# Feed-forward gate and up products as seven half-size products instead of eight, with the sums of weights on VectorE, and the down product in two groups

## The chip, the cores and the metric

The kernel runs on one core of a Trainium2 chip, as one program. The metric is device time in microseconds, lower is better. The engines are named as in the profile: PE is TensorE (its weight loads are listed as PEld), DVE is VectorE, ACT is ScalarE, POOL is GpSimd, SP issues the DMAs.

## The reference, cut to what matters

Two stacks of layers follow each other on 512 tokens of width 1024. They hold six feed-forward stages, two in the first stack (called ff0 and ff1 here) and four in the second (b0f1, b0f2, b1f1, b1f2), and between these mixers and a cross-attention. Only the feed-forward stages change.

```python
x = x + swiglu(rmsnorm(x, norm_ffn_g[layer]), ffn_w_gate_up[layer], ffn_w_down[layer])        # ff0, ff1
...
def _swiglu(h, w_gate, w_up, w_down):
    return (jax.nn.silu(h @ w_gate) * (h @ w_up)) @ w_down
...
x = x + 0.5 * _swiglu(_rmsnorm(x, ffn1_norm[i]), ffn1_w_gate[i], ffn1_w_up[i], ffn1_w_down[i])   # b0f1, b1f1
...
x = x + 0.5 * _swiglu(_rmsnorm(x, ffn2_norm[i]), ffn2_w_gate[i], ffn2_w_up[i], ffn2_w_down[i])   # b0f2, b1f2
```

The inner width is 2816 in all six, that is 22 column blocks of 128 for gate, 22 for up, and 22 blocks of rows for down.

## The kernel before

Rows are kept transposed: 8 chunks of 128 features by 512 tokens. A product in full precision is made of three matmuls: each operand is split into a rounded part and the rest (`split`, line 752: ScalarE makes the rounded copy `hi`, VectorE subtracts it to give `lo`), and hi by hi, hi by lo and lo by hi are summed in PSUM. The weights are split on the chip too: `weights` (line 765) loads a block of 128 x 8 x 128 floats (1024 columns per partition) into one of 3 tiles `raw`, then one ScalarE copy and one VectorE subtraction of 1024 columns fill two of the 6 tiles `part`.

`dense` (line 799) makes one column block: 8 chunks by 3 matmuls, each with 512 moving columns, so 24 matmuls. `ffn` (line 989) goes over the 22 inner blocks j: gate block j, then up block j, and in between `gate` for the block before, which scales both by the norm's factors, takes the silu, multiplies, and splits the result (4 VectorE instructions of 512 columns, the three products and the subtraction). The 22 pairs that come out are the operands of down: 8 column blocks of 22 x 3 = 66 matmuls, by `residual` (line 963), each added to a chunk of the rows by `add_product`. `prepare` (line 934) makes of every finished chunk what the next stage's norm takes from it. The last stage's down is `last_residual` (line 1025): its last column block goes by two halves of 256 tokens, so that the final norm of the first half runs under the products of the second.

The order of issue is not the order of the code. `Plan` collects the whole program and `schedule` (line 487) lists it anew, so that each engine takes the first instruction that could start by a model of the engines' times, with the tiles of each kind (line 655: 64 `blk` of 512 words, 3 `raw`, 6 `part`, 8 PSUM banks) as a limit. Each engine then runs its own list strictly in that order, waiting on semaphores. All instructions are issued from line 640 (in the changed kernel line 648), so rows are told apart by tile shape.

Of the kernel before, what the change touches and what calls it, by code (L numbers as in the profile page):

```python
# [28 lines left out]


# ---------------------------------------------------------------- host side: layout only
def _lay(w):
    """[K, N] -> [N/128, 128, K/128, 128]: one stationary column block per row of DRAM."""
    k, n = w.shape
    return np.ascontiguousarray(w.reshape(k // P, P, n // P, P).transpose(2, 1, 0, 3))


def _mov(w, kc):
    """[K, 512] -> [K/128/kc, 128, kc, 512]: moving blocks."""
    k, n = w.shape  # L40
    return np.ascontiguousarray(w.reshape(k // P // kc, kc, P, n).transpose(0, 2, 1, 3))

# [70 lines left out]
def _hyena_constants():  # L113
# [11 lines left out]
    # token order: even tokens, then odd ones  # L125
# [3 lines left out]
    # half-bin shifted frequencies: theta = 2 pi (f + 1/2) / 1024  # L129
# [4 lines left out]
    # forward: stationary [t, f]; [fc][128 t, (mat, kc), 128 f]  # L134
# [13 lines left out]
def pack(inputs):  # L148
# [9 lines left out]
    for l in range(2):  # L158
# [6 lines left out]
        a[f"ff_d{l}"] = _lay(g["ffn_w_down"][l])  # L165
# [66 lines left out]
class View:  # L232
    """A view of a Store, made when its memory is known; lo and hi bound the elements it can touch."""
# [64 lines left out]
class Plan:  # L298
    """Takes the program's instructions in an order that is right, and issues them in one in which each engine
    takes the first instruction, by that order, of those that could start, by a model of the engines' times.  # L300
    An instruction is taken ahead of others only where the tiles that it needs leave what is in front of it
    enough of them in any case."""
# [7 lines left out]
    def __init__(self, tc, kinds):  # L310
        """kinds: kind -> (pool, number of tiles, words per partition)"""
# [15 lines left out]
    def ahead(self, n=400):  # L327
        """what is added meanwhile comes before what it otherwise would by n instructions"""
# [30 lines left out]
    # ---- the program  # L359
# [47 lines left out]
    def _time(self, op, outs, ins):  # L407
        """microseconds on the engine"""
# [5 lines left out]
        if op.engine == "tensor":  # L414
# [3 lines left out]
            if rhs.dtype != F32:  # L418
                return 0.003 + max(size(rhs), 2 * P if rhs.dtype == F32R else 64) / 2400.0
# [18 lines left out]
    # ---- the order  # L438
# [2112 lines left out]
```

## Time and profile before

| | us |
|---|---|
| median of 3 runs | 3643.41 |
| lowest and highest run | 3643.01, 3643.46 |
| span of the profiled execution, first to last instruction | 3643.5 |
| PE busy in it | 3596.1 |
| DVE busy | 2042.3 |
| ACT busy | 1350.5 |
| POOL busy | 290.4 |

The profiled execution's own time is its span, 3643.5 us; nothing lies around it that the runs would count, since they agree with it within 0.5 us. Busy times count an instruction from its start to its end, and the starts of neighbours on one engine overlap the ends a little.

### The profile page before, as it was taken

To read this page: it belongs to the slowest core of one execution; us is meant where nothing else is said; L and a number is where in the kernel's file an instruction comes from. 1 tells how busy PE (TensorE), PEld (TensorE's weight loads), DVE (VectorE), ACT (ScalarE), POOL (GpSimd) and SP (SyncE) were. 2 spreads that over 40 slices of the span, in tenths; PEclk is the share of its full clock that TensorE was granted. 3 is DMA by queue.
4 is the path that set the end of the run, shared out by engine and by line. 5 is a ranking of instruction groups with operands and counts; after the bars stand their busy time and mean duration, and the time that the engine had idled before them with its cause. 6 is when DMAs were issued, how large, how long until landed. Compare 5 with 4: busy or idle time off the path is not lost. (4 is left out here: it accounts for less than half of the span.)

```text
span 3643.5 us, 46845 instructions
## 1 busy us (share of the span) xinstructions
PE 3596.1 (99%) x18186; PEld 2949.0 (81%) x18186; DVE 2042.3 (56%) x3262; ACT 1350.5 (37%) x2166; POOL 290.4 (8%) x358
## 2 busy tenths in 40 slices
PE   9999999999999999999999999999999999999998
PEld 6888888778788888887878888888888778888887
DVE  7664434466744345435887854434442787774433
ACT  4353223354532332222554442222322455443221
POOL 2010001000100010003210010000000330010000
PEclk9999999999999999999999999999999999999999
DMA  5323233233232322333425433333333432822232
GB/s 165 116 79 100 93 97 94 75 124 105 77 115 93 97 93 94 99 111 117 144 94 198 157 120 94 96 96 97 98 107 97 138 123 93 291 86 93 94 97 81
DMA packets 157654, 404.20 MB, mean 111 GB/s; under 512 B 17326, under 2 KB 40911, under 8 KB 157432
## 3 DMA queue, kind: packets, MB, share of 16 engines
q1 hardware_dynamic: 157432, 401.21, 34.6%
q8 instruction: 143, 2.34, 0.3%
q14 instruction: 79, 0.65, 0.1%
HBM read 375.46 MB, written 25.69 MB: 110 GB/s over the span
## 5 line engine op out<-in xcount | busy, mean ns | idle before, releaser
L640 PE MATMUL t<-t,t 128*128 128x512 f32 (+4 forms) x16892 | 3498.8, 367 | 28.4 <-ACT t L640 14.4
L640 PEld LDWEIGHTS t<-t,t 128*128 128x128 f32 (+1 forms) x15484 | 2766.9, 189 | 613.7 <-issue 28.5
L640 DVE TENSOR_TENSOR t<-t,t 128x512 f32<-128x512 f32 (+11 forms) x1831 | 1465.4, 813 | 1318.1 <-PE t L640 1102.9
L640 ACT CAST t<-t 128x1024 fp32r<-128x1024 f32 (+4 forms) x998 | 828.8, 841 | 1981.6 <-PE t L640 1481.6
L640 POOL TENSOR_TENSOR t<-t,t 128x512 f32<-128x512 f32 (+1 forms) x139 | 191.9, 1387 | 2169.6 <-ACT t L640 1806.6
L640 ACT ACTIVATE t<-t 128x512 f32<-128x512 f32 (+7 forms) x331 | 173.8, 534 | 79.4 <-DVE t L640 54.6
L640 DVE SCALAR_TENSOR_TENSOR t<-t,f,t 128x512 f32<-128x512 f32 (+2 forms) x209 | 155.8, 753 | 10.3 <-ACT t L640 7.1
L640 PE MATMUL t<-f,t 128*128 128x128 f32 (+2 forms) x1008 | 137.6, 258 | 11.0 <-DVE t L640 7.5
L640 PEld LDWEIGHTS t<-f,t 128*128 128x128 f32 (+1 forms) x880 | 113.1, 173 | 24.1 <-DVE t L640 6.9
L640 ACT COPY t<-t 128x512 f32<-128x512 f32 (+3 forms) x155 | 83.0, 558 | 109.4 <-PE t L640 107.4
L640 DVE SCALAR_TENSOR_TENSOR t<-f,f,t 128x512 fp32r<-128x512 f32 (+2 forms) x104 | 90.3, 885 | 52.4 <-ACT t L640 49.8
L640 POOL MEMSET t<- 128x2 f32 (+4 forms) x159 | 29.0, 214 | 1072.5 <-DVE t L640 540.7
L640 ACT ACTIVATE t<-t,t 128x128 f32<-128x128 f32 (+3 forms) x248 | 89.4, 435 | 42.9 <-PE t L640 26.6
L640 PEld LDWEIGHTS <-t 128*128 128x128 f16 (+1 forms) x1550 | 70.3, 98 | 40.6 <-issue 20.0
L640 DVE TENSOR_TENSOR f<-t,f 128x512 f32<-128x512 f32 x64 | 44.0, 688 | 56.6 <-PE t L640 56.6
L640 DVE SCALAR_TENSOR_TENSOR f<-t,f 128x512 f32<-128x512 f32 (+1 forms) x33 | 22.3, 676 | 94.2 <-PE t L640 94.2
L640 DVE SCALAR_TENSOR_TENSOR t<-t,t 128x4 f32<-128x4 f32 (+10 forms) x175 | 64.8, 377 | 13.3 <-ACT t L640 9.8
L640 ACT ACTIVATE t<-f 128x512 f32<-128x512 f32 (+1 forms) x105 | 64.4, 618 | 17.9 <-DVE f L640 17.2
L640 ACT ACTIVATE t<-t,f 128x512 f32<-128x512 f32 (+2 forms) x101 | 63.8, 657 | 13.2 <-PE t L640 10.8
L640 ACT ACTIVATE t<-f,f 128x512 fp32r<-128x512 f32 (+1 forms) x80 | 57.0, 718 | 29.0 <-DVE f L640 27.1
L640 DVE SCALAR_TENSOR_TENSOR t<-t,t,t 128x128 f32<-128x128 f32 x192 | 55.2, 345 | 11.8 <-PE t L640 8.5
L640 DVE TENSOR_TENSOR t<-t,f 128x512 f16<-128x512 f32 (+5 forms) x77 | 47.3, 623 | 5.7 <-PE t L640 5.2
(37 smaller groups left out, 421.2 us busy)
## 6 DMA issues: line engine op xcount, KB each, us to landing
t<-d SPq DMA_DIRECT2D x232, 256.0 KB, 4.7
t<-in_ffn_g SPq DMA_DIRECT2D x88, 512.0 KB, 3.5
t<-in_ffn_u SPq DMA_DIRECT2D x88, 512.0 KB, 3.4
t<-in_ffn_d SPq DMA_DIRECT2D x64, 512.0 KB, 3.6
t<-in_ff_g SPq DMA_DIRECT2D x44, 512.0 KB, 3.5
t<-in_ff_u SPq DMA_DIRECT2D x44, 512.0 KB, 3.5
d<-t SPq DMA_DIRECT2D x88, 256.0 KB, 3.3
t<-in_ff_d SPq DMA_DIRECT2D x32, 512.0 KB, 3.5
```

The lines of the kernel that those rows point to most:

```text
L640: ins = getattr(getattr(nc, o.engine), o.fn)(*[got(v) for v in o.args], **{k: got(v) for k, v in o.kw.items()})
```

## The change

The gate weights are taken two column blocks at a time, j and j + 11, together with the two halves of the 1024 features (chunks 0 to 3, and 4 to 7), and the tokens in two halves of 256 (`L` and `R`). A product of two such 2 x 2 arrangements of blocks takes eight block products when it is written out; here it is written with seven, of sums and differences of the blocks (the scheme is Strassen's, in Winograd's form). So `seven` issues 7 products of 4 chunks by 3 matmuls, 84 matmuls with 256 moving columns each, for what were two column blocks of 24 matmuls with 512 columns each. The same is done for up.

The sums on the side of the rows are made once per stage: `combine` makes 7 operands of chunk i and chunk i + 4. The sums of the weights are made for each pair of blocks by `combined_weights`: 4 additions of 512 columns on VectorE, and the split of 3584 columns where two blocks had 2048. Sums of the products: ScalarE copies four partial results out of PSUM, and VectorE adds them in `gate`. Down goes in two groups of inner rows, 12 blocks after j = 5 and 10 after j = 10 (`GROUPS`), each with its own 8 additions to the rows; its matmuls are the same ones as before. The host lays the rows of the down weights in the order in which the pairs come out (`_down`). There are 4 tiles `raw` in place of 3, and 63 `blk` in place of 64. The planner's time of a matmul has a new formula, so its lists change somewhat elsewhere too. Lines that are only comments are gone.

```diff
+GROUPS = [(0, 6), (6, 5)]
...
+def _down(w):
+    order = [k for i in range(FC // 2) for k in (i, FC // 2 + i)]
+    return np.ascontiguousarray(_lay(w)[:, :, order, :])
...
-            a[f"{f}_d{l}"] = _lay(g[f"{f}_w_down_2"][l])
+            a[f"{f}_d{l}"] = _down(g[f"{f}_w_down_2"][l])
...
-            "blk": (sb, 64, T), "raw": (sb, 3, 2 * T), "part": (sb, 6, 2 * T), "pad": (sb, 4, T + 16),
+            "blk": (sb, 63, T), "raw": (sb, 4, 2 * T), "part": (sb, 6, 2 * T), "pad": (sb, 4, T + 16),
...
-        if c == 0:
-            self.pre = {"xs": []}
+        if self.pre is None:
+            self.pre = {"xs": [None] * DC, "rows": {}}
...
-        if kind != "squares":
+        if kind == "xs":
             hi, lo = self.pair()
-            self.split_scaled(self.x[c], pre["g12"][:, c:c + 1] if kind == "twice" else self.col(g[0], g[1] + c), hi, lo)
-            pre["xs"].append((hi, lo))
+            self.split_scaled(self.x[c], self.col(g[0], g[1] + c), hi, lo)
+            pre["xs"][c] = hi, lo
+        elif kind != "squares":
+            row = pre["rows"][c] = self.blk()
+            nc.scalar.activation(out=row, in_=self.x[c], func=AF.Copy,
+                                 scale=pre["g12"][:, c:c + 1] if kind == "twice" else self.col(g[0], g[1] + c))
+            i = c % 4
+            if {i, i + 4} <= set(pre["rows"]):
+                pre["xs"][i] = self.combine(pre["rows"].pop(i), pre["rows"].pop(i + 4))
...
+    def combine(self, b1, b2):
+        nc = self.nc
+        L, R = slice(0, 256), slice(256, 512)
+        sub = lambda out, a, b: nc.vector.tensor_tensor(out=out, in0=a, in1=b, op=ALU.subtract)
+        minus = lambda out, a, b: nc.vector.scalar_tensor_tensor(out=out, in0=a, scalar=-1.0, in1=b, op0=ALU.mult,
+                                                                 op1=ALU.subtract)
+        one = self.blk(F32R)
+        self.split(b1[:, L], one[:, L], one[:, R])
+        low = self.pair()
+        self.split(b2, *low)
+        ta, tb = self.blk(), self.blk()
+        sub(ta[:, L], b1[:, L], b1[:, R])
+        minus(ta[:, R], b2[:, R], ta[:, L])
+        sub(tb[:, L], b2[:, R], b1[:, R])
+        minus(tb[:, R], ta[:, R], b2[:, L])
+        pa, pb = self.pair(), self.pair()
+        self.split(ta, *pa)
+        self.split(tb, *pb)
+        half = lambda pr, s: (pr[0][:, s], pr[1][:, s])
+        return [(one[:, L], one[:, R]), half(low, L), half(low, R), half(pb, R), half(pa, L), half(pa, R), half(pb, L)]
+    def combined_weights(self, a, b):
+        nc = self.nc
+        L, R = slice(0, T), slice(T, 2 * T)
+        ra, rb, s = (nc.tile("raw", (P, 2 * T)) for _ in range(3))
+        for r, src in ((ra, a), (rb, b)):
+            nc.sync.dma_start(out=r.rearrange("p (k n) -> p k n", n=P), in_=src)
+        add = lambda out, x, y: nc.vector.tensor_tensor(out=out, in0=x, in1=y, op=ALU.add)
+        def parts(src, n, kind="part"):
+            hi, lo = (nc.tile(kind, (P, n), F32R) for _ in range(2))
+            self.split(src, hi, lo)
+            return hi, lo
+        first = parts(ra, 2 * T)
+        add(s[:, R], ra[:, L], rb[:, L])
+        add(rb[:, L], rb[:, L], rb[:, R])
+        add(s[:, L], rb[:, L], ra[:, L])
+        third = parts(s, 2 * T)
+        second = parts(rb, 2 * T)
+        add(ra[:, R], ra[:, R], s[:, L])
+        last = parts(ra[:, R], T, "blk")
+        half = lambda pr, h: tuple(z[:, h].rearrange("p (k n) -> p k n", n=P) for z in pr)
+        return [half(first, L), half(first, R), half(last, L), half(second, R), half(second, L), half(third, L), half(third, R)]
+    def seven(self, w, xs, V, fresh):
+        nc = self.nc
+        bank = self.acc()
+        X, Z = bank[:, 0:256], bank[:, 256:512]
+        def product(out, n, start=False):
+            hi, lo = w[n]
+            mm = [(hi, k, z) for k in range(4) for z in xs[k][n]] + [(lo, k, xs[k][n][0]) for k in range(4)]
+            for i, (part, k, z) in enumerate(mm):
+                go = start and i == 0
+                nc.tensor.matmul(out, lhsT=part[:, k, :], rhs=z, start=go, stop=True, skip_group_check=not go)
+        ea, eb = self.blk(), self.blk()
+        e1, u2, u3, e5 = ea[:, 0:256], ea[:, 256:512], eb[:, 0:256], eb[:, 256:512]
+        product(X, 0, True)
+        nc.scalar.copy(out=e1, in_=X)
+        product(Z, 1)
+        product(X, 5)
+        nc.scalar.copy(out=u2, in_=X)
+        product(V, 4, fresh)
+        nc.scalar.copy(out=e5, in_=V)
+        product(X, 6)
+        nc.scalar.copy(out=u3, in_=X)
+        product(V, 2)
+        product(X, 3)
+        return Z, V, X, e1, u2, u3, e5
...
     def ffn(self, norm, wg, wu, wd, half):
         nc = self.nc
...
+        vt = nc.vector.tensor_tensor
+        minus = lambda out, a, b: nc.vector.scalar_tensor_tensor(out=out, in0=a, scalar=-1.0, in1=b, op0=ALU.mult, op1=ALU.mult)
+        L, R = slice(0, 256), slice(256, 512)
...
+        xs = self.pre["xs"][:4]
+        xs, factors = self.norm(*norm, xs=xs)
+        I = self.I
         rs = None
+        hidden = []
         def gate(G, U):
+            Z, V, X, e1, u2, u3, e5 = G
+            a, b = self.tmp(), self.tmp()
+            vt(out=a[:, L], in0=Z, in1=e1, op=ALU.add)
+            vt(out=a[:, R], in0=V, in1=u2, op=ALU.add)
+            minus(b[:, L], X, rs[:, L])
+            vt(out=b[:, R], in0=u3, in1=e5, op=ALU.add)
+            vt(out=a, in0=a, in1=rs, op=ALU.mult)
+            minus(b[:, R], b[:, R], rs[:, R])
+            for z in (a, b):
+                nc.scalar.activation(out=z, in_=z, func=AF.Silu)
+                vt(out=z, in0=z, in1=rs, op=ALU.mult)
+            Z, V, X, e1, u2, u3, e5 = U
+            h1, h2 = self.blk(), self.blk()
+            vt(out=h1[:, L], in0=Z, in1=e1, op=ALU.add)
+            vt(out=h1[:, R], in0=V, in1=u2, op=ALU.add)
+            minus(h2[:, L], X, b[:, L])
+            vt(out=h2[:, R], in0=u3, in1=e5, op=ALU.add)
+            vt(out=h1, in0=h1, in1=a, op=ALU.mult)
+            minus(h2[:, R], h2[:, R], b[:, R])
+            for z in (h1, h2):
+                pr = self.pair()
+                self.split(z, *pr)
+                hidden.append(pr)
+        def down(g):
+            i0, n = GROUPS[g]
+            ks = slice(2 * i0, 2 * i0 + 2 * n)
+            ys = list(hidden)
+            hidden.clear()
+            coming, self.coming = self.coming, self.coming if g else None
+            if g and self.out is not None:
+                self.last_residual(lambda c: I[wd][c][:, ks, :], ys, half)
+            else:
+                self.residual_with(lambda c: self.dense(None, c, ys, kmax=6, src=I[wd][c][:, ks, :]), half,
+                                   (0, 4, 1, 5, 2, 6, 3, 7))
+            self.coming = coming
+        last, bank = None, None
+        for j in range(FC // 2 + 1):
+            G = U = None
+            if j < FC // 2:
+                bank = self.acc()
+                G = self.seven(self.combined_weights(I[wg][j], I[wg][j + FC // 2]), xs, bank[:, L], True)
+                if j == 0:
+                    next(factors)
             if last is not None:
                 gate(*last)
+            if sum(GROUPS[0]) == j:
+                for _ in range(8):
+                    next(factors, None)
+                down(0)
+            if j < FC // 2:
+                U = self.seven(self.combined_weights(I[wu][j], I[wu][j + FC // 2]), xs, bank[:, R], False)
+                if j == 0:
+                    rs = next(factors)
+                else:
+                    for _ in range(2):
+                        next(factors, None)
+                last = G, U
+        down(1)
...
```

How this stands in the engines' lists. First DVE, in the middle of b0f1. Before, one inner block j takes these six rows (the three tiles with 1024 columns at their end belong to weights; t2177 holds the norm's factors):

```order
L640 TENSOR_TENSOR t2276_11240<-t2258_11139,t2268_11183 128x1024
L640 TENSOR_TENSOR t2279_11253<-t2271_11213,t2177_10655 128x512
L640 TENSOR_TENSOR t2281_11274<-t2265_11177,t2273_11217 128x1024
L640 TENSOR_TENSOR t2284_11287<-t2278_11251,t2177_10655 128x512
L640 TENSOR_TENSOR t2284_11287<-t2284_11287,t2279_11253 128x512
L640 TENSOR_TENSOR t2287_11304<-t2284_11287,t2286_11299 128x512
```

Of the change, in the same stage, from the third weight sum's subtraction (t2706, reading the tile `s`, t2699) to the use of the next set's second weight block (t2709, which SP loads into the tile that t2699 leaves, once t2706 is made):

```order
L648 TENSOR_TENSOR t2706_14240<-t2699_14185,t2703_14220 128x1024
L648 TENSOR_TENSOR t2708_14253<-t2692_14133,t2702_14208 128x1024
L648 TENSOR_TENSOR t2711_14268<-t2676_14007,t2704_14232 128x512
L648 TENSOR_TENSOR t2701_14194<-t2701_14194,t2633_13713 128x512
L648 TENSOR_TENSOR t2696_14149<-t2696_14149,t2633_13713 128x512
L648 TENSOR_TENSOR t2714_14292<-t2694_14142,t2713_14276 128x1024
L648 TENSOR_TENSOR t2716_14306<-t2694_14142,t2709_14257 128x512
L648 TENSOR_TENSOR t2701_14194<-t2701_14194,t2633_13713 128x512
L648 TENSOR_TENSOR t2709_14257<-t2709_14257 128x512
L648 TENSOR_TENSOR t2705_14235<-t2688_14111,t2691_14130 128x256
L648 TENSOR_TENSOR t2716_14306<-t2709_14257,t2694_14142 128x512
L648 SCALAR_TENSOR_TENSOR t2719_14339<-t2688_14111,t2696_14149 128x256
```

Where two subtractions of weights and four instructions of the gate made a block, 32 instructions now make a pair of blocks, 16 of them for weights, and weight sums and gate sums alternate.

Second, PE in the same place. Before, the first chunks of one column block (t2259 is the PSUM tile, t2244 the weights):

```order
L640 MATMUL t2259_11141<-t2043_9825,t2244_11039 128x512
L640 MATMUL t2259_11141<-t2045_9832,t2244_11039 128x512
L640 MATMUL t2259_11141<-t2057_9919,t2244_11039 128x512
L640 MATMUL t2259_11141<-t2059_9926,t2244_11039 128x512
L640 MATMUL t2259_11141<-t2071_10015,t2244_11039 128x512
```

Of the change, the first of seven products (t2677 is `hi` of the weights, from ScalarE, t2678 `lo`, from VectorE; a row with x2 is the two parts of one operand) and the start of the second:

```order
L648 MATMUL t2688_14111<-t2476_12977,t2677_14017 128x256 x2
L648 MATMUL t2688_14111<-t2504_13094,t2677_14017 128x256 x2
L648 MATMUL t2688_14111<-t2533_13219,t2677_14017 128x256 x2
L648 MATMUL t2688_14111<-t2561_13345,t2677_14017 128x256 x2
L648 MATMUL t2688_14111<-t2476_12977,t2678_14033 128x256
L648 MATMUL t2688_14111<-t2504_13094,t2678_14033 128x256
L648 MATMUL t2688_14111<-t2533_13219,t2678_14033 128x256
L648 MATMUL t2688_14111<-t2561_13345,t2678_14033 128x256
L648 MATMUL t2688_14111<-t2487_13027,t2677_14017 128x256
```

Each of the seven is twelve matmuls of half the width, eight with `hi` and then four with `lo`.

Third, DVE at the start of ff0, from the last chunks of the cross-attention's output on (f8 and f9 are chunks 6 and 7 of the rows). Before:

```order
L640 TENSOR_TENSOR f8_81<-t467_2176,f8_81 128x512
L640 TENSOR_TENSOR t477_2218<-t457_2141,t472_2196 128x1024
L640 TENSOR_TENSOR f9_82<-t474_2203,f9_82 128x512
L640 SCALAR_TENSOR_TENSOR t482_2237<-f8_81,f1_74,t476_2214 128x512
L640 SCALAR_TENSOR_TENSOR t485_2250<-f9_82,f1_74,t483_2242 128x512
L640 TENSOR_TENSOR t487_2260<-t464_2166,t475_2207 128x1024
```

Of the change, from behind the eighth matmul of the first product, up to the `lo` weights that its ninth reads (t498):

```order
L648 TENSOR_TENSOR t489_2259<-t482_2234,t486_2247 128x512
L648 SCALAR_TENSOR_TENSOR t457_2136<-t480_2226,t457_2136 128x256
L648 TENSOR_TENSOR t492_2267<-t480_2226,t488_2255 128x512
L648 TENSOR_TENSOR t494_2271<-t480_2226,t448_2107 128x256
L648 SCALAR_TENSOR_TENSOR t494_2271<-t457_2136,t480_2226 128x256
L648 TENSOR_TENSOR t495_2275<-t457_2136,t493_2269 128x512
L648 TENSOR_TENSOR f9_82<-t477_2214,f9_82 128x512
L648 TENSOR_TENSOR t454_2126<-t454_2126 128x512
L648 TENSOR_TENSOR t498_2283<-t445_2096,t465_2162 128x1024
```

Where one instruction prepared each chunk, `combine` now has nine for each pair of chunks, and two of the four pairs come due within the last chunks of the stage before.

## Rows read from the trace of the kernel before

**Rows 1.** The page: busy time of the engines, and their share in 40 slices of the span.
```profile
PE 3596.1 (99%) x18186; PEld 2949.0 (81%) x18186; DVE 2042.3 (56%) x3262; ACT 1350.5 (37%) x2166; POOL 290.4 (8%) x358
...
PE   9999999999999999999999999999999999999998
...
DVE  7664434466744345435887854434442787774433
```
**Rows 2.** What PE waited for, whole span: us in total, times, longest.
```profile
PE t L640 <- DVE t L640: 20.2, 24, 2.4
PE t L640 <- ACT t L640: 15.8, 19, 2.8
```
**Rows 3.** Windows: from:to, length, busy us (x instructions) by engine, clock, DMA.
```profile
400.00:500.00 100.00, 100.00 (x440) 82.24 (x439) 45.29 (x52) 29.98 (x37) 0.21 (x2) 1.00 0.32 98
1000.00:1100.00 100.00, 100.00 (x435) 81.37 (x434) 48.13 (x58) 32.16 (x39) 0.00 (x0) 1.00 0.35 111
1400.00:1500.00 100.00, 100.00 (x435) 81.34 (x434) 47.29 (x55) 29.31 (x36) 0.00 (x0) 1.00 0.29 95
2200.00:2300.00 100.00, 100.00 (x437) 81.85 (x437) 47.57 (x55) 29.76 (x38) 0.00 (x0) 1.00 0.32 98
2600.00:2700.00 100.00, 100.00 (x442) 82.58 (x441) 47.93 (x56) 30.24 (x38) 0.00 (x0) 1.00 0.31 95
3300.00:3400.00 100.00, 100.00 (x442) 82.58 (x441) 48.20 (x55) 29.30 (x36) 0.00 (x0) 1.00 0.29 95
```
**Rows 4.** Timeline of PE: one 256-column matmul, then runs of them (start, length).
```profile
204.17 0.37 PE L640 MATMUL t<-t,t 128*128 128x256 f32 x1
...
3618.09 6.18 PE L640 MATMUL t<-t,t 128*128 128x256 f32 x50
...
3624.70 3.24 PE L640 MATMUL t<-t,t 128*128 128x256 f32 x25
...
3628.14 3.68 PE L640 MATMUL t<-t,t 128*128 128x256 f32 x29
```
**Rows 5.** Timeline of DVE: two neighbours, then unbroken runs of equal instructions.
```profile
1718.98 0.69 DVE L640 TENSOR_TENSOR t<-t,t 128x512 f32<-128x512 f32 x1 [0.18 <-PE t L640]
1719.59 0.74 DVE L640 SCALAR_TENSOR_TENSOR t<-f,f,t 128x512 f32<-128x512 f32 x1
1720.25 2.49 DVE L640 TENSOR_TENSOR t<-t,t 128x512 fp32r<-128x512 f32 x4
...
1951.45 2.36 DVE L640 TENSOR_TENSOR t<-t,t 128x1024 fp32r<-128x1024 f32 x2
...
2011.04 1.09 DVE L640 TENSOR_TENSOR t<-t 128x256 f32<-128x256 f32 x3
```
**Rows 6.** Groups by shape in b0f1's gate and up, 1310 to 1556 us.
```profile
L640 DVE TENSOR_TENSOR t<-t,t 128x1024 fp32r<-128x1024 f32 x43 | 53.6, 1249 | 73.3 <-PE t L640 69.2 <-ACT t L640 4.1
L640 ACT CAST t<-t 128x1024 fp32r<-128x1024 f32 x44 | 46.3, 1053 | 154.0 <-PE t L640 141.2 <-issue 12.7
L640 ACT ACTIVATE t<-t 128x512 f32<-128x512 f32 x20 | 12.5, 624 | 5.1 <-DVE t L640 5.1
L640 ACT CAST t<-t 128x512 fp32r<-128x512 f32 x19 | 11.8, 621 | 9.1 <-DVE t L640 9.1
```
**Rows 7.** DMA issues in the same stretch: count, KB each, median us to landing.
```profile
t<-in_ffn_u SPq DMA_DIRECT2D x22, 512.0 KB, 3.4
t<-in_ffn_g SPq DMA_DIRECT2D x21, 512.0 KB, 3.5
```
**Rows 8.** Windows outside the feed-forward stages in which DVE is busiest.
```profile
1700.00:1800.00 100.00, 94.85 (x442) 73.34 (x442) 87.54 (x150) 50.60 (x83) 34.87 (x43) 1.00 0.35 117
2000.00:2100.00 100.00, 93.76 (x634) 86.43 (x633) 83.31 (x206) 49.68 (x139) 1.30 (x1) 0.95 0.50 167
2900.00:3000.00 100.00, 98.23 (x733) 79.86 (x732) 86.72 (x163) 58.27 (x91) 28.66 (x45) 1.00 0.37 124
```
**Rows 9.** Windows: gate and up of ff0 and of ff1, from their first load on.
```profile
227.00:460.00 233.00, 231.89 (x1022) 190.28 (x1021) 120.06 (x145) 75.86 (x96) 8.28 (x6) 1.00 0.32 100
948.00:1189.00 241.00, 238.67 (x1030) 192.84 (x1029) 131.65 (x171) 84.07 (x106) 9.61 (x8) 0.99 0.33 104
```
**Rows 10.** Timeline of DVE at the end: the norm of the two halves.
```profile
3628.42 3.22 DVE L640 SCALAR_TENSOR_TENSOR t<-f,f,t 128x256 f32<-128x256 f32 x8 [1.22 <-PE t L640]
3631.85 0.42 DVE L640 SCALAR_TENSOR_TENSOR f<-t,f 128x256 f32<-128x256 f32 x1 [0.21 <-PE t L640]
...
3637.29 3.22 DVE L640 SCALAR_TENSOR_TENSOR t<-f,f,t 128x256 f32<-128x256 f32 x8 [1.31 <-PE t L640]
```

More of the change, by code (lines that the diff above doesn't have):

```diff
@@ L964, in residual, with residual_with @@
         self.residual_with(lambda c: self.dense(wname, c, ys, order=order), half)
-    def residual_with(self, product, half):
+    def residual_with(self, product, half, order=range(DC)):
         last = None
-        for c in range(DC):
+        for c in order:
             acc = product(c)
-            if c:
-                self.add_product(c - 1, last, half)
-            last = acc
+            if last is not None:
+                self.add_product(*last, half)
+            last = c, acc
             if self.side is not None:
                 next(self.side, None)
-        self.add_product(DC - 1, last, half)
+        self.add_product(*last, half)
     def add_product(self, c, acc, half, tokens=None):
@@ L1018, in ffn @@
-            last = G, U
-        gate(*last)
-        if self.out is not None:
-            self.last_residual(wd, a, half)
-        else:
-            self.residual(wd, a, half)
-    def last_residual(self, wname, ys, half):
+            if sum(GROUPS[0]) == j:
[10 more added lines that the diff above has]
+                last = G, U
@@ L1028, in last_residual @@
+        down(1)
+    def last_residual(self, weights, ys, half):
         nc = self.nc
@@ L1030, in last_residual, with parts, product @@
         last = None
+        kc = len(ys)
+        def parts(c):
+            return [(k, self.weights(weights(c)[:, k:min(k + 5, kc), :], min(k + 5, kc) - k)) for k in range(0, kc, 5)]
+        def product(out, ws, s):
+            for k0, (hi, lo) in ws:
+                self.mm3s(out, [((hi[:, k, :], lo[:, k, :]), tuple(z[:, s] for z in ys[k0 + k])) for k in range(min(5, kc - k0))],
+                          k0 == 0, k0 + 5 >= kc)
         for c in range(DC - 1):
-            acc = self.dense(wname, c, ys)
+            acc = self.acc()
+            product(acc, parts(c), slice(0, T))
             if c:
@@ L1036, in last_residual @@
         c = DC - 1
-        kc = len(ys)
-        parts = [(k, self.weights(self.I[wname][c][:, k:min(k + 8, kc), :], min(k + 8, kc) - k)) for k in range(0, kc, 8)]
+        w = parts(c)
         self.add_product(c - 1, last, half)
@@ L1042, in last_residual @@
             acc = self.acc()[:, :256]
-            for k0, (hi, lo) in parts:
-                self.mm3s(acc, [((hi[:, k, :], lo[:, k, :]), tuple(z[:, s] for z in ys[k0 + k])) for k in range(min(8, kc - k0))],
-                          k0 == 0, k0 + 8 >= kc)
+            product(acc, w, s)
             with nc.ahead():
@@ L2487, in _coming @@
     if s[2:] in ("f1", "f2"):
-        return "xs", f"ffn{s[3]}_norm_2", int(s[1]) * DC
+        return "xc", f"ffn{s[3]}_norm_2", int(s[1]) * DC
     return ("squares",)
```

46 lines of the change are left out of this document (16 added, 30 removed).

## The prediction

> **What bounds the kernel now.** I read the page first. PE is busy 99% of the span, in every slice but the last, and DVE 56% [rows 1]. Then the waits: PE waited 20.2 us for DVE and 15.8 us for ACT in the whole execution [rows 2]. So the time is the sum of PE's instructions, and an edit helps if it shortens that sum and keeps PE fed. Then six stretches from inside the six gate and up parts: PE is at 100%, DVE at 45 to 48%, ACT at 30%, and the clock at its full level of 2.4 GHz [rows 3]. There PE issues 435 to 442 matmuls of 512 columns in 100 us, on average 438.5, one in 0.228 us.
>
> I count in pairs: two inner blocks, gate and up. There are 11 pairs in a stage and 66 in the kernel. Before, a pair is 2 x 2 x 24 = 96 matmuls of 0.228 us, 21.9 us of PE.
>
> **PE's work.** A pair becomes 2 x 84 = 168 matmuls of 256 columns. Their price stands in the last column block, which already goes by halves. A matmul alone lasts 0.37 us, and a run of 50 lasts 6.18 us, so one starts every (6.18 - 0.37) / 49 = 0.119 us; the runs of 25 and 29 give 0.120 and 0.118 [rows 4]. That is more than half of 0.228: each matmul pays some columns' time whatever its width, and the change pays it 1.75 times as often. A pair is then 168 x 0.119 = 20.0 us. The 512-column rate spreads by 1.6% between stages [rows 3]; the same spread here gives 19.8 to 20.3. The floor of PE falls by 1.9 us a pair, 125 us in all. Down has the same matmuls as before and saves nothing.
>
> The Trainium skill, "TensorE: Matmul & The Clock Gate", section "Back-to-back issue gap", gives N / 2.4 + 2.5 ns, which would be 109 ns for 256 columns and 216 ns for 512, and by it a pair would go from 20.7 to 18.4 us, a saving of 2.4 us. The rows show 119 and 228 ns, so I take 1.9.
>
> **DVE's work.** A neighbour starts 0.61 us after the start of an instruction that lasts 0.69, so an unbroken run ends about 0.08 us later than its last share. Runs of two, four and three then give 1.135 us for 1024 columns, 0.60 for 512 and 0.337 for 256 [rows 5]. Before, a pair cost 4 subtractions of weights and 8 instructions of the gate: 4 x 1.135 + 8 x 0.60 = 9.3 us of 21.9. After, the weights of gate and of up each take three subtractions of 1024, one of 512 and four sums of 512: 6 x 1.135 + 10 x 0.60 = 12.8 us for both. The gate has six instructions of 512 columns and ten of 256: 3.6 + 3.4 = 7.0 us. Together 19.8 us against PE's 20.0. That doubles DVE, and it is the whole risk. The sums in 256 columns with a constant (the `minus` lines) have no row of their own; the nearest, 0.337, is taken, and at the 512-column price they would add at most 1.1 us a pair.
>
> **ACT** rounds 6 x 1.05 us of weights, 2 x 0.62 more, two silus and two roundings of 0.62 each [rows 6], and copies eight pieces of 256 columns out of PSUM, for which no row stands; they cost between nothing and the 0.62 of a 512-column instruction. That is 10 to 15 us of 20: no bound, but each copy stands between two products that share `X` or `V`. Another product of 12 x 0.119 = 1.4 us lies between them and covers a copy of half a microsecond, even behind part of a rounding of 1.05.
>
> **How far PE and DVE can drift apart.** The six `part` tiles hold one set of weights. A tile pair that is last read in the fifth of seven products (7.1 us into a set of 10) is read again in the third product of the next set (at 12.9). In these 5.7 us ACT needs 1.05 and DVE 1.14, so DVE may come some 3 us early or late before PE waits. Within a group of six pairs DVE also starts with its first set done under the stage before, and the gate of the last pair falls under down: it has some 106 us of work (6 x 19.8 less 6.4 and 7.0) for 120 us of PE, but it can use only those 3 us or so of lead. What it loses within a set, waiting for a rounding or a load, it can hardly make up. The second weight block of a set is loaded into the tile that the third sum's subtraction leaves. DVE then has 1.14 + 3 x 0.60 + 1.14 = 4.1 us of other work by its list, and a load lands 3.4 to 3.5 us after its issue [rows 7]: covered, with 0.6 us to spare. If that cover is gone, DVE waits, and then PE. In the same stage before, DVE also waited for ACT, 4.1 us over 43 of the subtractions [rows 6], 0.1 us each.
>
> I take a pair at 20.5 us: the 20.0 of PE, 0.2 for the spread of rates, 0.3 for waits behind DVE. That gives 66 x 1.4 = 92 us. The bounds are 19.8 (DVE's sum alone, PE at its best) and 22.6 (below).
>
> **What the change adds.** At the start of ff0 and ff1 the stage before is short. DVE has there, by its list, from behind the eighth matmul of the first product to the `lo` that the ninth reads, 4 x 0.60 + 3 x 0.337 + 0.60 + 1.14 = 5.1 us, with nothing else for PE. Another 1 us goes for the last chunk's operands. In their gate and up parts PE was idle 1.1 and 2.3 us before [rows 9], mostly at that place, so the net is about 4.4 us each: 9 us. A clock that falls in the gap could add some: in the stretch in which PE was idle for 6.2 us, the mean granted clock was 0.95 [rows 8]. The four other stages start behind products of 5 us and more a column block; there the last chunk's operands (an addition, a ScalarE pass, a rounding, signals) come about 2.8 us after the last product, and two products of half width cover most of that: 1.5 us each, 6 us. Where a group of down begins or ends, PE changes to tiles that the others have just left: 1 us a stage, 6 us. Down's 8 more additions lie on a DVE that is idle there. At the end, the second half's products shrink from 66 matmuls to 30, and the first half's norm, 3.22 us of DVE [rows 10], lies less under them: 2 us. In all 23 us, between 8 and 45.
>
> **Sum.** 3643.5 - 92 + 23 = 3574.5, against an execution that agrees with the median of the runs.
>
> **The rivals.**
> PE at its floor: DVE's lead hides all its waits, and a pair takes 20.0 us or a little less. For it speaks the 5.7 us window; against it that both engines would be at 99%. 3643.5 - 125 + 23 = 3541; 0.14. If the matmuls of 256 columns came faster than 0.119, DVE would bound, at 19.8: 3643.5 - 139 + 23 = 3528. The rows speak against it, 0.02. The formula of the Trainium skill's page on TensorE, named above, would lead there.
>
> DVE paces: it waits 1.2 us a pair for roundings and loads, so the pair takes 21.0 to 21.2. 3643.5 - 53 + 23 = 3614. For it speaks that each engine keeps its list's order and that each of the eight splits of a pair's weights waits for a rounding; 0.17.
>
> Slower than before: DVE can't be kept busier here than where it is busiest now, 83 to 88% in stretches in which PE itself fell to 94 to 98% [rows 8]. 19.8 / 0.875 = 22.6 us a pair, 66 x 0.7 = 46 us lost, and 3643.5 + 46 + 23 = 3713. The point from which it decides is 21.9 - 23 / 66 = 21.55 us a pair, a DVE share of 92%. Against it: those stretches are chains of small dependent instructions; here 16 of 32 depend on weights alone. 0.09.
>
> **How the numbers follow.** The likeliest is a pair of 20.2 to 20.9 us, that is 3554 to 3600 us, 0.54; PE's floor 0.16 with its faster case; DVE pacing 0.17; too little to tell from none, 0.04; slower 0.09. A measurement of this kernel tells 0.2%, 7 us, from no change. The range 3540 to 3640 takes in the likeliest, the DVE-paced case, and half of PE's floor. Faster 0.87, same 0.04, slower 0.09.
>
> **What would show it.** In a stretch of 100 us inside gate and up there should be 810 to 830 matmuls of 256 columns (840 at the floor) and DVE 94 to 98% busy, against 46% now. Waits of PE for DVE should be a few tenths a pair; 1 us a pair or more is DVE pacing, and then the row just ahead of DVE's idle time tells whether a rounding or a load held it. Runs of 256 columns at 0.119 us a start show PE's term; ff0 and ff1 should show one gap of 4 to 6 us each ahead of the ninth matmul. I am wrong if DVE's share stays under 92%, if the 256-column matmuls next to a busy DVE start slower than 0.125 us apart, or if down, which I leave as it is, loses time at its group borders.

## The result and the profile after

The change made the kernel slower: a median of 3675.31 us (four runs, 3669.09 to 3677.46) beside 3643.43 us, ratio 1.008 with a 95% interval of 1.0066 to 1.0094. I had forecast 3575 us, and gave "slower" 9 in 100.

The page of the changed kernel, as in [rows 1]:

```profile
PE 3531.5 (96%) x22902; PEld 3098.9 (84%) x22902; DVE 2820.3 (77%) x4822; ACT 1777.0 (48%) x3102; POOL 313.9 (9%) x358
...
PE   9989999999899999999999999999999999999998
...
DVE  7689596466995989595887898588867888789685
```

PE's busy time fell by 65 us, and the span grew by 32. So PE now stands idle 144 us, where it was 47 us. What it waited for (total us, times, longest), as in [rows 2]:

```profile
PE t L648 <- ACT t L648: 100.1, 158, 8.9
PE t L648 <- DVE t L648: 26.9, 33, 4.1
```

Waits for VectorE, which I had called "the whole risk", grew by 7 us. Waits for ScalarE grew from 16 to 100 us. Windows inside gate and up, cut so that nearly all matmuls in them have 256 columns (length, busy us and instructions by engine, clock, DMA), beside [rows 3]:

```profile
300.00:360.00 60.00, 57.69 (x477) 56.67 (x476) 57.43 (x94) 34.65 (x58) 0.00 (x0) 1.00 0.27 89
1380.00:1450.00 70.00, 67.23 (x554) 66.01 (x553) 66.89 (x106) 39.28 (x66) 0.00 (x0) 1.00 0.29 94
2190.00:2260.00 70.00, 66.77 (x552) 65.34 (x551) 66.74 (x105) 40.15 (x67) 0.00 (x0) 1.00 0.31 98
3330.00:3400.00 70.00, 67.22 (x557) 66.00 (x556) 66.18 (x107) 40.64 (x68) 0.00 (x0) 1.00 0.28 91
```

That is 2140 matmuls in 270 us, 793 in 100 us where I had 810 to 830, one in 0.126 us, with PE 96% and DVE 95% busy. A pair takes 168 x 0.126 = 21.2 us. I had 20.5. The timeline of PE in one such stretch, and of ACT at the same place (start, length; in brackets the idle time ahead and what ended it):

```profile
304.75 2.92 PE L648 MATMUL t<-t,t 128*128 128x256 f32 x23
308.13 10.74 PE L648 MATMUL t<-t,t 128*128 128x256 f32 x88 [0.46 <-ACT t L648]
319.33 2.87 PE L648 MATMUL t<-t,t 128*128 128x256 f32 x22 [0.46 <-ACT t L648]
...
307.70 0.37 ACT L648 COPY t<-t 128x256 f32<-128x256 f32 x1 [1.02 <-PE t L648]
```

The run of 88 goes at (10.74 - 0.37) / 87 = 0.119 us a start, as [rows 4] had it. It is broken about once a set of 84, here right behind a copy of 256 columns by ScalarE. Which copy, the order of issue tells. Four rows of PE's list at one set of the changed kernel (t_4822 is the PSUM tile with `X` and `Z`; behind the arrow stand the moving operand and the weights; `Activation_49` is the semaphore that counts what ScalarE has done):

```
L648 MATMUL t_4822<-t_2153,t_4741 128x256
L648 MATMUL t_4822<-t_2183,t_4727 128x256
L648 MATMUL t_4822<-t_2199,t_4727 128x256
L648 MATMUL t_4822<-t_2232,t_4727 128x256 [waits Activation_49]
```

The first row is the last of the first product, into `X`; the second row is the first of the second product, into `Z`, the other half of the same bank. The third matmul of `Z`, the last row, waits for the copy of `X`. So the product that was to cover the copy waits for it. The timelines above show the turns that they take: PE's run ends at 307.67 us, the copy goes from 307.70 to 308.07, and PE starts again at 308.13.

The start of ff0, same view:

```profile
227.52 4.37 POOL L648 TENSOR_TENSOR t<-t,t 128x512 f32<-128x512 f32 x3 [68.83 <-ACT t L648]
229.21 3.22 DVE L648 TENSOR_TENSOR t<-t,t 128x256 fp32r<-128x256 f32 x2
...
243.49 4.91 POOL L648 TENSOR_TENSOR t<-t,t 128x512 f32<-128x512 f32 x2 [7.40 <-ACT t L648]
...
247.20 2.28 DVE L648 TENSOR_TENSOR t<-t,t 128x1024 fp32r<-128x1024 f32 x1
248.45 0.58 PE L648 MATMUL t<-t,t 128*128 128x256 f32 x1 [8.89 <-ACT t L648]
249.54 6.34 PE L648 MATMUL t<-t,t 128*128 128x256 f32 x31 [0.50 <-DVE t L648]
```

PE is idle for 9 us, behind the eighth matmul as forecast, where I had 5.1 and 1 us. Two subtractions of 256 columns take 3.22 us, and one of 1024 takes 2.28 us, where [rows 5] have two in 2.36 us; both lie beside GpSimd's additions. Those are the sums of squares for the next norm. Behind the gap the clock is lower (windows, clock in the third column from the end):

```profile
248.40:255.50 7.10, 6.54 (x31) 6.25 (x32) 7.10 (x9) 4.33 (x7) 1.35 (x2) 0.54 0.01 2
255.50:265.70 10.20, 9.68 (x83) 9.48 (x82) 9.10 (x19) 5.16 (x10) 0.00 (x0) 1.00 0.33 103
```

0.54 is near the lower of the two levels, 1.2 of 2.4 GHz; before it PE had waited 9 us.

Two more readings answer to those of before. The loads of gate weights land in 4.1 us in place of 3.5 [rows 7], which VectorE hardly feels: from 1400 to 1500 us it waited 0.2 us for one. From the last addition to the rows to the end of the span, 13.8 us are left (3675.5 - 3661.66), where it was 11.7 (3643.5 - 3631.85) [rows 10]: the second half's norm now stands behind a part of the first half's, and the 2 us that the prediction had for the end came out.

```profile
t<-in_ffn_g SPq DMA_DIRECT2D x88, 512.0 KB, 4.1
t<-in_ffn_u SPq DMA_DIRECT2D x88, 512.0 KB, 3.6
```
```profile
3661.66 0.42 DVE L648 SCALAR_TENSOR_TENSOR f<-t,f 128x256 f32<-128x256 f32 x1
...
3668.80 3.22 DVE L648 SCALAR_TENSOR_TENSOR t<-f,f,t 128x256 f32<-128x256 f32 x8 [1.32 <-PE t L648]
```

### The profile page after: what moved, and what is told of

Its sections match the earlier page's. It is cut to its first block, busy times and chain, and to the rows that moved or that the text cites. A ratio compares the mean times of both kernels' runs of the same rounds, so it can differ in the third digit from the quotient of the medians.

```text
span 3675.5 us, 58890 instructions
## 1 busy us (share of the span) xinstructions
PE 3531.5 (96%) x22902; PEld 3098.9 (84%) x22902; DVE 2820.3 (77%) x4822; ACT 1777.0 (48%) x3102; POOL 313.9 (9%) x358
## 5 line engine op out<-in xcount | busy, mean ns | idle before, releaser
L648 PE MATMUL t<-t,t 128*128 128x256 f32 (+4 forms) x21608 | 3429.5, 319 | 119.1 <-ACT t L648 97.9
L648 PEld LDWEIGHTS t<-t,t 128*128 128x128 f32 x20200 | 2918.3, 191 | 488.2 <-ACT t L648 136.3
L648 DVE TENSOR_TENSOR t<-t,t 128x512 f32<-128x512 f32 (+7 forms) x2791 | 2009.3, 761 | 550.4 <-PE t L648 397.8
L648 ACT CAST t<-t 128x1024 fp32r<-128x1024 f32 (+4 forms) x1406 | 1084.0, 798 | 1165.4 <-PE t L648 869.5
L648 ACT COPY t<-t 128x256 f32<-128x256 f32 (+2 forms) x683 | 280.3, 414 | 489.7 <-PE t L648 488.2
L648 DVE SCALAR_TENSOR_TENSOR t<-t,t 128x256 f32<-128x256 f32 (+7 forms) x487 | 210.8, 438 | 21.0 <-ACT t L648 17.8
L648 ACT ACTIVATE t<-t 128x512 f32<-128x512 f32 (+8 forms) x331 | 172.9, 537 | 101.7 <-DVE t L648 74.4
L648 DVE TENSOR_TENSOR t<-t 128x256 f32<-128x256 f32 (+2 forms) x367 | 198.5, 548 | 13.3 <-ACT t L648 9.1
L648 DVE SCALAR_TENSOR_TENSOR t<-f,f,t 128x512 fp32r<-128x512 f32 (+2 forms) x64 | 52.0, 836 | 29.1 <-ACT t L648 27.3
L648 ACT ACTIVATE t<-f,f 128x512 f32<-128x512 f32 (+1 forms) x80 | 56.9, 719 | 22.9 <-DVE f L648 21.4
```

The costliest lines, as they stand in the source:

```text
L648: ins = getattr(getattr(nc, o.engine), o.fn)(*[got(v) for v in o.args], **{k: got(v) for k, v in o.kw.items()})
```

## The experiments

All times in us; the ratio is to the kernel before, run on the same chip (its medians there 3645.68 to 3647.83, and 3643.43 beside the changed kernel, so a difference between versions that ran on different chips can be off by some 4 us). no_sums and before_no_sums leave a part of the work out: ahead of the feed-forward stages the norm's total is then that of the first chunk alone.

| run | median | lowest to highest | ratio, 95% interval |
|---|---|---|---|
| x_bank | 3600.31 | 3593.90 to 3603.49 | 0.9857 to 0.9886 |
| order_xa | 3672.88 | 3668.44 to 3676.99 | 1.0054 to 1.0088 |
| before_groups | 3654.33 | 3651.50 to 3658.17 | 1.0015 to 1.0033 |
| x_bank_order | 3597.91 | 3594.02 to 3602.23 | 0.9853 to 0.9882 |
| no_sums | 3562.36 | 3559.89 to 3565.20 | 0.9754 to 0.9783 |
| before_no_sums | 3638.05 | 3631.46 to 3639.47 | 0.9963 to 0.9982 |
| fillers | 3604.21 | 3601.39 to 3611.91 | 0.9871 to 0.9901 |
| pe_sums | 3599.03 | 3593.70 to 3604.27 | 0.9855 to 0.9885 |
| dve_sums | 3570.42 | 3566.38 to 3573.10 | 0.9776 to 0.9809 |
| pe_sums_order | 3598.94 | 3593.70 to 3604.24 | 0.9855 to 0.9885 |
| after_dve_sums | 3649.89 | 3645.41 to 3656.05 | 1.0000 to 1.0018 |
| before_dve_sums | 3639.98 | 3635.98 to 3644.68 | 0.9971 to 0.9990 |
| dve_sums_order | 3570.57 | 3567.81 to 3572.84 | 0.9775 to 0.9804 |

**x_bank: `Z` leaves the bank of `X`.**

```diff
-    def seven(self, w, xs, V, fresh):
+    def seven(self, w, xs, X, fresh):
-        X, Z = bank[:, 0:256], bank[:, 256:512]
+        V, Z = bank[:, 0:256], bank[:, 256:512]
-        product(X, 0, True)
+        product(X, 0, fresh)
-        product(Z, 1)
+        product(Z, 1, True)
-        product(V, 4, fresh)
+        product(V, 4)
```

> The changed kernel with Z moved out of the bank of X into that of V, so that gate and up share a bank for X; the same products in the same order. Theory (false wait): Z waits once a set for ScalarE's copy of X, since the two halves of a bank are one tile to what sets the waits. In the changed kernel PE then has one gap of about 0.62 us a set, 132 sets, 82 us. With Z elsewhere the copy lies under Z's product: about 3593 us (3580 to 3610), PE's waits for ACT fall from 100 us to under 30, 820 or more matmuls of 256 columns in 100 us. Rival (VectorE paces): VectorE is 88 to 96% busy already, so the gap only passes from ACT to DVE: 3645 to 3675 us, PE's waits for DVE rise from 27 to 80 us or more.

75 us less than the changed kernel, and 1.3% less than before, inside the theory's range. Its waits, a run of PE and its windows:

```profile
PE t L648 <- DVE t L648: 34.2, 33, 4.8
PE t L648 <- ACT t L648: 27.9, 36, 3.1
```
```profile
299.81 30.45 PE L648 MATMUL t<-t,t 128*128 128x256 f32 x254
```
```profile
300.00:360.00 60.00, 59.95 (x503) 59.64 (x502) 59.95 (x98) 36.43 (x61) 0.00 (x0) 1.00 0.33 106
1360.00:1440.00 80.00, 79.83 (x670) 79.51 (x669) 79.95 (x128) 47.47 (x78) 0.00 (x0) 1.00 0.32 106
2150.00:2220.00 70.00, 70.00 (x587) 69.65 (x586) 69.36 (x112) 41.53 (x70) 0.00 (x0) 1.00 0.33 106
3250.00:3340.00 90.00, 89.94 (x754) 89.51 (x754) 89.23 (x144) 55.18 (x92) 0.00 (x0) 1.00 0.32 106
```

254 matmuls stand in one run, with no break. The windows hold 2514 in 300 us, 0.1193 us each, so a pair takes 20.05 us; and DVE is busy for 298.5 of the 300 us without holding PE up. The rival is out: PE's waits for ScalarE fell by 72 us, and those for VectorE rose by 7, where the rival had them rise by 50 or more. 66 x (21.2 - 20.05) = 76 us, which is the gain.

The expectation called the wait false. That is not quite so. The Trainium skill, "PSUM — Partial Sum Buffer", section "PSUM bank collisions raise a hardware error", says that two engines must not access one bank in the same partitions at once, even at different columns, and that PSUM has to be guarded by bank, not by address. No run here tried a kernel without the guard. By that rule a wait like that of the list's last row is needed where the halves share a bank, and the arrangement is what has to change, as here.

**order_xa and x_bank_order: the column blocks ahead of ff0 and ff1.**

```diff
-        self.residual(f"xa_o{l}", os_)
+        self.residual_with(lambda c: self.dense(f"xa_o{l}", c, os_), False, (0, 4, 1, 5, 2, 6, 3, 7))
```

> The changed kernel with one edit: the output of cross-attention, ahead of ff0 and ff1, goes by column blocks 0, 4, 1, 5, 2, 6, 3, 7 in place of 0 to 7, so that the first combination can start after the second block and not after the fifth. Theory (chain of combinations): the gaps of 9.05 and 8.36 us are VectorE's work on the four combinations, about 5 us each, of which three come in the last four blocks; in the new order the gaps fall to 4 to 5 us, and the stretches at half clock behind them may shrink: 10 to 15 us in all, 3660 to 3665. Rival (the gap is the latency of the last combination alone, or of the square sums on GpSimd): gaps of 8 to 9 us stay, the time within 4 us of 3675.

> Both edits, Z beside V and the new order of column blocks ahead of ff0 and ff1. Theory: they add up, since one acts inside the sets and the other at two starts: 10 to 15 us under the first alone, about 3580 us (3565 to 3600). Rival (with the waits for copies gone, VectorE paces, and what the starts lose less comes back as waits for VectorE within the first group): the same as with Z beside V alone, within 4 us.

Neither is told from the same kernel in the old order (3672.9 beside 3675.3, 3597.9 beside 3600.3, with ranges that overlap). The gaps did change: the longest wait for ScalarE fell from 8.9 to 3.9 us,

```profile
PE t L648 <- ACT t L648: 85.7, 155, 3.9
```

but it came apart into several shorter ones. From 205 to 272 us PE is idle 7.3 us in order_xa and 9.9 in the changed kernel, and at ff1 (920 to 1020 us) 10.7 and 12.1. So the gaps shrank about as the theory had it, and the time stayed as the rival had it: the order of the blocks is worth no more than the 2 us that can't be told from none.

**before_groups: down in two groups, alone.** The kernel before with the operands of down taken after 12 inner blocks and again after 10, with loads of 6 inner blocks (5 in the last stage).

```diff
+            if j == 12:
...
+                down(0)
...
-            self.residual(wd, a, half)
+        down(1)
```

> The kernel before, with gate and up as there, and only down cut into two groups of 12 and 10 inner blocks, with loads of 6 inner blocks (5 in the last stage). Theory (down's groups cost little): 8 more additions a stage on an idle VectorE and two more changes of tiles, 0 to 8 us: 3643 to 3652. Rival (the borders of the groups cost several us a stage, and are a part of the 147 us by which the changed kernel misses PE's floor): 3660 or more.

8.7 us more: just above the theory's range, far from the rival.

**no_sums and before_no_sums: no squares on GpSimd.**

```diff
-            else:
+            elif kind not in ("xc", "twice"):
                 nc.gpsimd.tensor_tensor(out=pre[n], in0=pre[n], in1=sq, op=ALU.add)
```

> The kernel with Z beside V, and without GpSimd's additions of the squares ahead of the six FFN stages (the norm's total is then the first chunk's squares alone; nothing else is left out). Theory (GpSimd slows VectorE at the starts): at the six starts VectorE's instructions that lie beside such an addition last up to 1.1 us longer, 4 to 9 us a start, 39 us in all; the start's chain of combinations runs on VectorE, so PE's gaps of about 40 us at the starts halve: 3570 to 3585. Rival (the chain and the latencies alone make the gaps): within 5 us of 3600.

> The kernel before, with the same additions of squares left out (the norm's total is the first chunk's squares alone). Control for the run without sums. Theory: VectorE's instructions are stretched there too, but PE has products enough at the starts, with gaps of 4 us in all: 3640 to 3646. Rival (the additions cost the same in any kernel): 3630 or less.

38 us less beside `Z` with `V`, more than expected, and 10 us less in the kernel before, between the two theories. So about 28 us of the price belong to the change. At ff0 the two kinds of subtraction are short again, and PE's longest gap is 2.6 us, where it is 4.8 in x_bank and was 8.9 in the changed kernel:

```profile
228.51 1.02 DVE L648 TENSOR_TENSOR t<-t,t 128x256 fp32r<-128x256 f32 x2
...
244.91 1.22 DVE L648 TENSOR_TENSOR t<-t,t 128x1024 fp32r<-128x1024 f32 x1
...
243.18 0.39 PE L648 MATMUL t<-t,t 128*128 128x256 f32 x1 [0.19 <-DVE t L648]
246.19 16.17 PE L648 MATMUL t<-t,t 128*128 128x256 f32 x103 [2.62 <-DVE t L648]
```

**fillers: products that nothing reads, in the gaps of the starts.** On the kernel with `Z` beside `V`.

```diff
+        filler = self.acc()
+        for _ in range(14 if wg[:2] == "ff" and wg[2] == "_" else 6):
+            nc.tensor.matmul(filler[:, 0:256], lhsT=self.ident, rhs=self.x[7][:, 0:256], start=True, stop=True)
```

> The kernel with Z beside V, and at each of the six starts products that nothing reads (14 of 256 columns at ff0 and ff1, 6 at the others, fp32), which by the list stand where PE would wait for the last combination. Theory (the clock): the granted clock is at 1.2 GHz for about 55 us behind the gaps of the starts since PE stood idle; with PE busy in the gaps it stays at 2.4 GHz, and the products there go at full rate: 3580 to 3590. Rival (the fillers lie in the path, since the data are there earlier than the list thinks, or the clock falls anyway): 3600 to 3615.

3604 beside 3600 us: no gain. But the clock did rise. The stretch behind ff0's gap with fillers, and then without them, in x_bank:

```profile
248.40:255.50 7.10, 6.68 (x36) 5.63 (x35) 7.10 (x12) 4.09 (x6) 1.34 (x1) 0.98 0.00 0
```
```profile
248.40:257.00 8.60, 6.18 (x28) 5.89 (x29) 8.60 (x13) 5.49 (x8) 4.20 (x2) 0.52 0.03 6
```

In both VectorE is busy throughout, so a faster PE had little to win there. That the fillers delayed the products behind them by what the clock gave back can't be excluded: at ff0 their run (14 products, 28 rows) lasts 7.89 us, and the next run of products starts at 253.15 us, where it starts at 250.71 in x_bank. As a way to win time they are out.

**pe_sums, dve_sums, pe_sums_order and dve_sums_order: the sums on another engine.** All with `Z` beside `V`. In pe_sums each square goes through products with a column of ones into one PSUM tile; dve_sums has one edit:

```diff
-                nc.gpsimd.tensor_tensor(out=pre[n], in0=pre[n], in1=sq, op=ALU.add)
+                (nc.vector if kind in ("xc", "twice") else nc.gpsimd).tensor_tensor(out=pre[n], in0=pre[n], in1=sq, op=ALU.add)
```

> The kernel with Z beside V, and the squares ahead of the six FFN stages summed by PE in place of GpSimd: for each chunk four products of its square with a column of ones, gathered in one PSUM tile, 28 more of them a total than the four that stand there now, seven totals in all. Theory (GpSimd's additions stretch VectorE at the starts): the gain of leaving the sums out stays, less the price of 196 small products of about 0.1 us, 20 us where none falls in a gap of PE: 3570 to 3585. Rival (the small products wait for ScalarE's squares in PE's order and open gaps of their own): 3595 to 3610.

> The kernel with Z beside V, and the additions of the squares ahead of the six FFN stages on VectorE in place of GpSimd. Theory: 49 additions of 512 columns at 0.60 us, 29 us of VectorE, take the place of 39 us by which its instructions were stretched; they need not lie in the chain: 3580 to 3595. Rival (VectorE has no room at the starts or behind them, so each addition delays PE): 3598 to 3615.

> Sums on PE, Z beside V, and cross-attention's output ahead of ff0 and ff1 by column blocks 0, 4, 1, 5, 2, 6, 3, 7. Theory (with nothing to stretch VectorE, its four combinations of 5 us in the last four blocks of 2.7 us are what is left of the gaps of ff0 and ff1, 3 to 5 us each): 4 to 8 us under the same kernel in the old order. Rival (what is left is the latency of the last combination): within 3 us of it.

> Z beside V, sums on VectorE, and cross-attention's output ahead of ff0 and ff1 by column blocks 0, 4, 1, 5, 2, 6, 3, 7. Theory (PE's gaps that are left, some 19 us at ff0 and ff1, are VectorE's four combinations in the last four blocks): 5 to 10 us under the same kernel in the old order, 3560 to 3566. Rival (they are the latency of the last combination, or VectorE has too much work there in any order): within 4 us of 3570.

dve_sums is the fastest version that does the whole work, 3570.4 us, ratio 0.9792 (below the expected 3580 to 3595): 49 additions more on VectorE cost less than the stretch that GpSimd's cause. The pages of x_bank, no_sums and dve_sums show both:

```profile
PE 3511.7 (98%) x22902; PEld 3094.8 (86%) x22902; DVE 2806.4 (78%) x4822; ACT 1775.1 (49%) x3102; POOL 320.9 (9%) x358
```
```profile
PE 3496.5 (98%) x22902; PEld 3084.6 (87%) x22902; DVE 2760.6 (78%) x4822; ACT 1773.5 (50%) x3102; POOL 221.7 (6%) x309
```
```profile
PE 3500.8 (98%) x22902; PEld 3084.3 (86%) x22902; DVE 2784.2 (78%) x4871; ACT 1771.6 (50%) x3102; POOL 220.7 (6%) x309
```

The same 4822 instructions keep VectorE busy 46 us less without GpSimd's additions, and the 49 additions then add 24 us.

pe_sums gains nothing, though PE has no gap at ff0 any more. The small products in x_bank and in pe_sums, as groups:

```profile
L648 PE MATMUL t<-f,t 128*128 128x1 f32 x332 | 43.7, 247 | 6.8 <-POOL t L648 4.9 <-ACT t L648 1.7
```
```profile
L648 PE MATMUL t<-f,t 128*128 128x1 f32 x724 | 91.4, 242 | 4.5 <-POOL t L648 2.5 <-ACT t L648 2.0
```

392 rows more, two for each of the 196 products, where my price had one: 3599.0 - 3562.4 = 37 us, 0.09 a row if the rows are the whole difference; in the trace neighbouring ones start 0.10 us apart. That is what leaving GpSimd out had given. In neither did the order of the blocks add anything.

**after_dve_sums and before_dve_sums: the two losses one by one.** The same edit in the changed kernel as it was, and in the kernel before.

> The changed kernel as it is, with Z in the bank of X, and only the additions of the squares ahead of the six FFN stages moved from GpSimd to VectorE. Theory (two separate losses, the copy's wait inside the sets and the stretched VectorE at the starts): the gain is as large as beside the other edit, 30 us of 3675: 3638 to 3652, and the waits of 0.62 us a set stay. Rival (the two losses share a cause, or the starts of this kernel wait for something else): 3660 or more.

> The kernel before with the same additions on VectorE. Theory: PE has products enough at its starts, so there is little to win, no more than the 10 us that leaving the additions out gave: 3638 to 3648. Rival (the edit is worth 30 us in any kernel, and has nothing to do with this change): 3625 or less.

25 us less in the changed kernel, which makes it level with the kernel before, within 0.2%; 7 us less in the kernel before. Moving `Z` alone gives 75 us, moving the sums alone 25, both 105: two separate losses that nearly add up. The stretch itself, over all subtractions of 256 columns of a kernel (count, total, mean ns), in the changed kernel and in dve_sums:

```profile
L648 DVE TENSOR_TENSOR t<-t,t 128x256 fp32r<-128x256 f32 x36 | 24.7, 695 | 22.1 <-PE t L648 14.3 <-ACT t L648 7.7
```
```profile
L648 DVE TENSOR_TENSOR t<-t,t 128x256 fp32r<-128x256 f32 x36 | 14.9, 420 | 20.2 <-PE t L648 14.4 <-ACT t L648 5.7
```

The Trainium skill, "SBUF — State Buffer", section "Who interferes with whom", says that a VectorE instruction with two inputs in SBUF contends with a GpSimd instruction that reads SBUF, for ports that both share. The trace agrees. The 695 ns are a mean of two kinds: ten of the 36 run beside an addition of GpSimd and take 0.98 to 1.53 us, and the other 26 take 0.42 or so, as all 36 do in dve_sums, where none runs beside one. The subtraction of 1024 columns is 1.06 us longer beside one (2.28 against 1.22). How the two engines share out the time, no run shows.

## Why the prediction was wrong, by its own steps

**The step that failed.** "[...] each copy stands between two products that share `X` or `V`. Another product of 12 x 0.119 = 1.4 us lies between them and covers a copy of half a microsecond [...]" For three of four copies this held. Behind the first copy the covering product is `Z`'s, and `Z` shares the bank of `X`; the prediction counted the tiles that share data and not those that share a bank. By the windows' rates the wait costs (21.2 - 20.05) / 2 = 0.58 us a set, 76 us in 132 sets; x_bank put it at 75 us. The price of a pair in the sum was 20.5, almost half a microsecond over what x_bank shows, so of the 101 us between 3574.5 and the measured time the pair has 66 x (21.2 - 20.5) = 46. The other 55 lie in the additions: 3675.3 - 3643.4 + 66 x (21.9 - 21.2) = 78 us, where the sum had 23.

**The starts.** For ff0 and ff1 I worked out 5.1 us of VectorE from the durations of unstretched rows [rows 5]; at the starts GpSimd adds squares at the same time. after_dve_sums puts that at 25 us for all six starts, before_dve_sums at 7 in the kernel before, where, as I take it, PE had products enough. In the stretches of [rows 9] PE is idle 15.8 and 16.8 us in the changed kernel (the copy's waits among them), 10.8 and 10.0 in x_bank, 4.7 and 10.6 in dve_sums, and 1.1 and 2.3 before. So with both losses gone my "4.4 us each" comes out at ff0 (3.6) and not at ff1 (8.3). Of the four other starts, which the prediction puts behind "products of 5 us and more a column block", two stand behind a mixer, whose last eight additions come 4 us apart in the kernel before. The windows of dve_sums, of x_bank, and of the changed kernel:

```profile
227.00:460.00 233.00, 228.30 (x1565) 211.86 (x1564) 189.09 (x312) 120.00 (x195) 0.00 (x0) 0.99 0.34 102
948.00:1189.00 241.00, 230.39 (x1591) 213.66 (x1589) 198.64 (x329) 119.15 (x190) 0.00 (x0) 0.99 0.32 95
```
```profile
227.00:460.00 233.00, 222.17 (x1490) 205.92 (x1489) 182.89 (x292) 113.95 (x184) 16.18 (x7) 0.96 0.31 99
948.00:1189.00 241.00, 230.98 (x1568) 213.22 (x1567) 200.71 (x326) 123.06 (x197) 16.61 (x7) 0.98 0.33 100
```
```profile
227.00:460.00 233.00, 217.21 (x1466) 199.98 (x1465) 181.87 (x285) 111.95 (x179) 11.69 (x7) 0.98 0.31 96
948.00:1189.00 241.00, 224.22 (x1467) 204.40 (x1466) 194.45 (x316) 118.64 (x192) 14.34 (x7) 0.96 0.31 95
```

**PE's work: right.** 0.119 us a matmul and 20.0 us a pair; x_bank has 0.1193 and 20.05. The formula of the Trainium skill's page that the prediction weighed, 109 ns, is shown by no run; the page gives it for a matmul by itself, and says that a stream with weight loads goes otherwise. (By the formula a pair would take 18.3 us, not the 18.4 that stands there.)

**VectorE's work: right in size, the risk misjudged.** 19.8 us a pair were forecast, and DVE is 99.5% busy in x_bank. I took 0.3 us a pair for waits behind it, and gave 0.26 in all to rivals in which it paces or can't pass 87%. Neither happened: in x_bank it fills 99.5% and PE loses 0.05 us a pair. That the pair came out at 21.2, the price of the rival in which VectorE paces, is chance: what held PE was the copy. The slower rival named the outcome, and by the wrong mechanism; its deciding point, 21.55 us a pair, was not even reached (21.2), and the kernel was slower all the same, since the additions were 78 us and not 23.

**The additions: 23 us forecast, about 49 found without the two losses.** 3643.4 - 66 x (21.9 - 20.05) = 3521, and dve_sums takes 3570. The traces place them roughly, if each execution is cut where VectorE makes the last addition to the rows of a stage. By the rates every feed-forward stage should be 11 x (21.9 - 20.05) = 20 us shorter than before. In dve_sums ff0 and ff1 are 7 and 11 us short of that, and the four others 8 together; the end is 2 us longer; and 18 us lie outside the six stages, 12 of them in the two mixers ahead of b0f2 and b1f2 (24 in the changed kernel). For these the sum had no term, though the planner's new times changed their lists too; no run tells what makes them longer. Down's groups cost 8.7 us by before_groups, where the prediction had 6 at the borders. But by the same cuts its six stages are together some 4 us shorter than before, and its two mixers 11 us longer, so a price of the borders themselves is not shown.

**Settled and open.** That the copy's wait and GpSimd's sums make the changed kernel slower is shown, since each was taken away with the expected sign, alone and together, and for the sums with a control in the kernel before. What is left at ff0 and ff1 is open: it is not the order of the column blocks, and products that keep the clock up don't win it back. Why the mixers became longer is open too.

## What to carry to other kernels

Before a short operation is called covered, look at what the covering work shares with it: in this kernel's waits a PSUM bank counted as one thing, whichever columns were used, and 0.58 us a turn, seen only as PE at 96% in place of 99.9%, cost 75 us in 132 turns. A duration is good only for the neighbours it was measured with: the price of a VectorE instruction from a stretch in which GpSimd is idle doesn't hold where GpSimd works. An engine at 99% needn't hold the other one up. Here half of its work depended on loaded weights alone; that this is the reason was not tested.

## What the runs showed of the hardware that I had not expected

VectorE ran at 99.5% over 300 us beside a PE at 99.9%. GpSimd's addition of 512 columns made a neighbouring VectorE instruction about 1.1 us longer (2.28 against 1.22 us for 1024 columns, 1.53 against 0.42 for 256), and 49 such additions were cheaper on the busy VectorE than on the idle GpSimd by 30 us (3570.4 against 3600.3). A product of fp32 with a single column shows as two rows of PE, 0.10 us from start to start.
